# Layer 1 of a hybrid decoder: where k's last sums of squares and the pairs' preparation stand among the projections

## The chip, the cores and the metric

The kernel runs on one core of one Trainium2 chip. The metric is the device time of one execution in microseconds (us). Engines are named as the profile names them: PE multiplies matrices (PEld is its loading of weights), DVE, ACT and POOL work elementwise on the on-chip memory, SP issues the transfers between that memory and the chip's main memory. Each engine takes its instructions in one fixed order; an instruction that waits holds all that stands behind it on its engine.

## What is computed

The reference is a trunk of two layers over 512 tokens of width 2048, in float32. The change lies in layer 1, whose first part is this:

```python
xr = x + xx * mu[0]; xk = x + xx * mu[2]; xg = x + xx * mu[5]   # also xw, xv, xa; xx is the token before, minus x
r = (xr @ w_r); k = (xk @ w_k); v = (xv @ w_v); g = (xg @ w_g)
w_log = -softplus(-(w0 + tanh(xw @ w1) @ w2)) - 0.5
decay = exp(-exp(w_log))
a = sigmoid(a0 + (xa @ a1) @ a2)
kk = (k * k_k).reshape(B_, S, H, N)
kk = kk / max(sqrt(sum(kk * kk, axis=-1)), L2_EPS)
k = k * (1.0 + (a - 1.0) * k_a)
o = wkv7_scan(r, decay, k, v, kk, a)      # 32 heads of 64
bonus = sum(r * k * r_k, axis=-1) * v
```

A norm over o, a gate with silu(g), an output projection and a layer norm follow.

## The kernel before

Every float32 matrix is held as two parts: a rounded one (`hi`, made by ACT, L137) and the rest (`lo`, made by DVE, L138). A product of two such matrices is three PE products (L142 to L144).

**Projections.** `gemm_a` makes 256 columns of a projection (a block): four units of weights, each 512 KB, loaded into `wraw` and split into `whi` and `wlo`, and for each of the 16 slices of x 2 x 3 products of 128x512, so 96 products in a block. The two halves of a block collect in two accumulators `ga` and are taken out by the function `evac` at its end. After each of the four units `pump()` takes one piece of other work from the list `self.side`. k, r and g take eight blocks each, in that order; then v's projection runs inside the scan.

**Mixes.** Each projection reads its own mixture of x with the token before (`mx`, 16 tiles, one buffer each). A mixture is two steps on ACT and two on DVE in turn: scale (L599), add (L600), round (L137), rest (L138). The tiles of the next projection take the buffers of the last one, so mixture i for r can be written only when k's last block has read its own mixture i. With `feed` they are made in the first block of a projection as written, and ahead of it where the engines have time.

**k.** For each half block (a pair of heads, 16 in all) `ev_k` copies the accumulator to `spill`, stores it, squares it (`sq`), splits the square (`sqr`), and puts on the side list a piece that adds it with two products into `ssq`, one row for each head. `self.flush()` runs what is left of the list when k's blocks are written. Beside k's blocks lie two more things: the first factors of w and a (`low`, `loa`, from mixtures `ml`), and `token_layout`, 16 pieces in which POOL scales and shifts a tile of layer 0's output (`xr`, L666 and L667) for a later stage; they are held back until the block before them has been taken out (`gate`).

**Preparation.** After `ssq` DVE makes 1/norm (`rsykk`), stores it as `rn_d`, and `prep(p)` prepares the scan's operands of one pair: it loads k, the norm and the weights `w2`, splits the weights (`w2h`), makes six products (`prew`, `prea`), and goes through ACT and DVE (from `pL`, the running sum, to `rkr`) to two results, which are stored as `ar_d` and `bk_d`. A second part, after `yield`, adds two products (`pb`) and stores `bc_d`. All of its tiles lie in the pool `gph`.

**Order.** The framework's scheduler sets the order on every engine, by what is ready in its own reckoning and by the order in which the code is written; in the scan PE's order is that of the code.

Of the kernel before, what the change touches and what calls it, by code (L numbers as in the profile page):

```python
# [8 lines left out]
F32 = mybir.dt.float32  # L9
# [8 lines left out]
P = 128  # L18
S = 512
# [15 lines left out]
class Kernel:  # L35
# [568 lines left out]
    def layer1(self, x1, x1_ctx, xhat_d, x1_d):  # L604

        nc, tc, i = self.nc, self.tc, self.i
# [22 lines left out]
        hid, lps = {}, {}  # L629
        with tc.tile_pool(name="kph", bufs=1) as kp:  # L630
# [37 lines left out]
                nc.sync.dma_start(x1_d[t * P:(t + 1) * P, sl], r)  # L668

            for c in range(8):  # L670
                if c > 1:
                    with tc.issue_after(gate[0].ins):
                        for q in range((c - 2) * 16 // 6, (c - 1) * 16 // 6):
                            token_layout(q % 4, q // 4)
                self.gemm_a(i["od_w_k"][0], c * 256, m, lambda n, ps: ev_k(c, n, ps), feed=feed)
                ks = [k for k in range(NK) if k * 6 // NK == c]
                for nm, j, w in (("w", 1, i["od_w1"][0]), ("a", 4, i["od_a1"][0])):
                    if not ks:
                        continue
                    nk = len(ks)  # L680
                    wr = kp.tile([P, 3, 96], F32, tag="l1r", name="l1r")[:, :nk]
                    nc.sync.dma_start(wr, w[ks[0] * P:(ks[-1] + 1) * P, :].rearrange("(k p) n -> p k n", p=P))
                    wh = kp.tile([P, 2, 3, 96], F32R, tag="l1h", name="l1h", bufs=2)[:, :, :nk]
                    self.split(wh[:, 0], wh[:, 1], wr)

                    def add(ks=ks, nm=nm, wh=wh, ml=list(self.mixes(kp, tp, x1, j, ks, "ml", 5))):
                        for kk, k in enumerate(ks):
                            self.mm3(lps[nm], wh[:, 0, kk, :], wh[:, 1, kk, :], ml[kk][:, 0, :], ml[kk][:, 1, :],
                                     k == 0, k == NK - 1)

                    self.side.append(add)
            self.flush()
            for nm in "wa":
                h = hid[nm] = hp.tile([96, 2, S], F32R, name="hid" + nm)
                if nm == "w":
                    t = tp.tile([96, S], F32, tag="sp", name="th", bufs=2)
                    nc.scalar.activation(t, lps[nm], AF.Tanh)
                    self.split(h[:, 0, :], h[:, 1, :], t)
                else:
                    self.split(h[:, 0, :], h[:, 1, :], lps[nm])  # L700
            m, feed = [], self.mixes(mp, tp, x1, 0)
            for h in range(2):
                sl = slice(h * 256, h * 256 + 256)
                sm = kp.tile([32, 256], F32, tag="ssm", name="ssm")
                nc.vector.tensor_scalar(sm, ss[:32, sl], 1e-30, None, ALU.max)
                rn = self.rsqrt(kp, sm, 0.0, 256, f"kk{h}", rows=32)
                nc.vector.tensor_scalar(rn, rn, 1.0 / L2_EPS, None, ALU.min)
                nc.sync.dma_start(rn_d[:, sl], rn)
        with tc.tile_pool(name="gph", bufs=1) as gp:

            rt = {}

            def ev_r(p, ps):
                rt[p] = gp.tile([P, S], F32, tag="pr", name="pr", bufs=3)
                nc.scalar.copy(rt[p], ps)

            last = None
            for c in range(8):
                self.gemm_a(i["od_w_r"][0], c * 256, m, lambda n, ps: ev_r(2 * c + n, ps), feed=feed)
                for p in (2 * c, 2 * c + 1):  # L720
                    pr = self.prep(gp, p, rt[p], hid, k_d, rn_d, ar_d, bk_d, bc_d)
                    self.side += [lambda pr=pr: next(pr), lambda pr=last: pr and next(pr, None)]
                    last = pr

            m, feed = [], self.mixes(mp, tp, x1, 5)

            def ev_g(c, n, ps):
                th = tp.tile([P, S], F32, tag="sp", name="gth", bufs=2)
                nc.scalar.activation(th, ps, AF.Tanh, scale=0.5)
                nc.vector.scalar_tensor_tensor(th, th, 1.0, ps, ALU.add, ALU.mult)  # L730
                nc.sync.dma_start(g_d[2 * c + n], th)

            wg = i["od_w_g"][0]
            self.side.append(lambda: next(last, None))
            self.gemm_a(wg, 0, m, lambda n, ps: ev_g(0, n, ps), feed=feed)
            self.flush()
        swp = self.lctx.enter_context(tc.tile_pool(name="swp", bufs=2, side="right"))
        ld_ctx = self.ctx.enter_context(ExitStack())
        ld = ld_ctx.enter_context(tc.tile_pool(name="ld", bufs=1, side="right"))
        for c in range(1, 8):  # L740
            self.gemm_a(wg, c * 256, m, lambda n, ps: ev_g(c, n, ps))
        xv, feed = [], self.mixes(mp, tp, x1, 3)
        self.ps_ctx.close()
        self.wp, self.ww = swp, 512
# [12 lines left out]
    def prep(self, tp, p, r, hid, k_d, rn_d, ar_d, bk_d, bc_d):  # L757
# [30 lines left out]
        iP = tw  # L788
        nc.scalar.activation(iP, L, AF.Exp, scale=CE)
        nc.gpsimd.tensor_copy(self.pcs[:, p, :].unsqueeze(2), Pi[:, :, 64:65])  # L790
        AR, BK = T("pAR", "pAR", (P, 8, 2, 64), 2), T("pBK", "pBK", (P, 8, 2, 64), 2)

        nc.vector.scalar_tensor_tensor(rn, k, col(self.hv["kk"]), rn, ALU.mult, ALU.mult)
        ia, ir = p % 2, 1 - p % 2
# [513 lines left out]
```

## Time and profile before

| | |
|---|---|
| median of 3 runs | 2136.67 us (2131.53 to 2141.84) |
| the profiled execution | 2133.83 us, its span 2132.1 us |
| PE / DVE / ACT / POOL busy | 96 / 61 / 45 / 13 % of the span |
| k's blocks, r's blocks, g's blocks | about 817 to 1014.5, 1014.5 to 1238.5, 1238.5 to 1420 us |
| scan | from about 1424 us |

A busy PE says little, since products overlap: one lasts 0.39 us and the next starts 0.23 us after it. How many products a stretch holds says more.

### The profile page before, as it was taken

The page shows a single profiled execution, that of the slowest core. Times are in us where ns is not written, and L with a number is a line of the kernel's source. Part 1 is how long each engine was busy: PE and PEld are TensorE (multiplying, and loading weights), DVE is VectorE, ACT ScalarE, POOL GpSimd, SP SyncE. Part 2 cuts the span into 40 slices and gives each one's busy share as a digit, 9 for nine tenths or more (in the row PEclk, how much of TensorE's full clock was granted, in tenths as well). Part 3 has the DMA queues.
Part 4 walks back from the last instruction along what each step waited for, and adds up shares of the span by engine and source line. Part 5 has one row for each costly group of instructions (what it writes and reads, how often), then busy time and mean ns, then how long its engine had stood idle before and what let it go on. Part 6 is the DMA issues. An engine that isn't in the chain of part 4 may idle for free. (4 is left out here: it accounts for less than half of the span.)

```text
span 2132.1 us, 33773 instructions
## 1 busy us (share of the span) xinstructions
PE 2036.6 (96%) x13139; PEld 1645.7 (77%) x13139; DVE 1301.0 (61%) x2557; ACT 954.4 (45%) x1663; POOL 268.9 (13%) x334
## 2 busy tenths in 40 slices
PE   8999999999999998999899989999999999989996
PEld 7888888888888897777688768876667676666786
DVE  5334335445333358666777793368888988987336
ACT  3345345333221138555555672254555555564211
POOL 0000000000000000333000030012333333310003
PEclk9999999999999999999999999999999999999998
DMA  5322222333333343455466665322222332333733
GB/s 190 99 70 79 82 77 65 94 99 99 99 105 113 127 170 123 147 177 157 130 235 215 211 210 189 122 80 63 91 87 89 105 104 68 104 109 100 232 104 114
DMA packets 214031, 262.97 MB, mean 123 GB/s; under 512 B 15768, under 2 KB 161776, under 8 KB 213104
## 3 DMA queue, kind: packets, MB, share of 16 engines
q1 hardware_dynamic: 213872, 260.83, 37.6%
q8 instruction: 103, 1.69, 0.3%
q14 instruction: 56, 0.46, 0.1%
HBM read 214.32 MB, written 46.47 MB: 122 GB/s over the span
## 5 line engine op out<-in xcount | busy, mean ns | idle before, releaser
L138 DVE TENSOR_TENSOR wlo<-wraw,whi 128x1024 fp32r<-128x1024 f32 (+1 forms) x268 | 313.8, 1173 | 487.5 <-ACT whi L137 478.5
L137 ACT CAST whi<-wraw 128x1024 fp32r<-128x1024 f32 (+1 forms) x324 | 303.5, 938 | 563.8 <-PE ga L143 318.7
L143 PE MATMUL ga<-mx,whi 128*128 128x512 f32 x768 | 301.9, 393 | 4.1 <-DVE mx L138 4.1
L142 PE MATMUL ga<-mx,whi 128*128 128x512 f32 x768 | 301.1, 393 | 4.5 <-ACT mx L137 4.5
L142 PE MATMUL ga<-x,whi 128*128 128x512 f32 x768 | 301.0, 392 | 0.0
L144 PE MATMUL ga<-mx,wlo 128*128 128x512 f32 x768 | 301.0, 392 | 0.0
L144 PE MATMUL ga<-x,wlo 128*128 128x512 f32 x768 | 299.5, 390 | 0.4 <-DVE wlo L138 0.4
L143 PE MATMUL ga<-x,whi 128*128 128x512 f32 x768 | 299.1, 390 | 0.0
L490 PE MATMUL gb<-wlo,mixed 128*128 128x512 f32 (+1 forms) x576 | 196.8, 343 | 3.1 <-DVE wlo L138 3.1
L488 PE MATMUL gb<-whi,mixed 128*128 128x512 f32 (+1 forms) x576 | 197.4, 343 | 1.8 <-DVE s L439 1.8
L489 PE MATMUL gb<-whi,mixed 128*128 128x512 f32 (+1 forms) x576 | 196.9, 342 | 0.0
L143 PEld LDWEIGHTS ga<-mx,whi 128*128 128x128 f32 x768 | 145.4, 189 | 38.0 <-DVE mx L138 6.9
L142 PEld LDWEIGHTS ga<-mx,whi 128*128 128x128 f32 x768 | 145.1, 189 | 37.9 <-ACT mx L137 5.9
L144 PEld LDWEIGHTS ga<-mx,wlo 128*128 128x128 f32 x768 | 145.3, 189 | 30.9 <-issue 0.3
L144 PEld LDWEIGHTS ga<-x,wlo 128*128 128x128 f32 x768 | 144.2, 188 | 31.2 <-DVE wlo L138 0.9
L142 PEld LDWEIGHTS ga<-x,whi 128*128 128x128 f32 x768 | 144.3, 188 | 29.4 <-ACT whi L137 0.3
L143 PEld LDWEIGHTS ga<-x,whi 128*128 128x128 f32 x768 | 144.3, 188 | 29.1
L490 PEld LDWEIGHTS gb<-wlo,mixed 128*128 128x128 f32 x576 | 109.1, 190 | 16.8 <-DVE wlo L138 4.4
L488 PEld LDWEIGHTS gb<-whi,mixed 128*128 128x128 f32 x576 | 109.1, 190 | 16.0 <-DVE s L439 3.5
L489 PEld LDWEIGHTS gb<-whi,mixed 128*128 128x128 f32 x576 | 109.2, 190 | 12.4
L142 PE MATMUL vps<-mx,whi 128*128 128x512 f32 x256 | 113.3, 443 | 0.0
L138 POOL TENSOR_TENSOR wlo<-wraw,whi 128x512 fp32r<-128x512 f32 x56 | 74.4, 1328 | 256.6 <-ACT whi L137 234.2
(330 smaller groups left out, 3401.0 us busy)
## 6 DMA issues: line engine op xcount, KB each, us to landing
wraw<-in_ev_w_in SPq DMA_DIRECT2D x96, 512.0 KB, 3.6
wraw<-in_ev_w_out SPq DMA_DIRECT2D x32, 512.0 KB, 3.6
wraw<-in_od_w_k SPq DMA_DIRECT2D x32, 512.0 KB, 4.9
wraw<-in_od_w_r SPq DMA_DIRECT2D x32, 512.0 KB, 4.5
wraw<-in_od_w_g SPq DMA_DIRECT2D x32, 512.0 KB, 3.4
wraw<-in_od_w_v SPq DMA_DIRECT2D x64, 256.0 KB, 2.8
ar_d<-pAR SPq DMA_DIRECT2D x16, 512.0 KB, 2.6
bk_d<-pBK SPq DMA_DIRECT2D x16, 512.0 KB, 3.3
```

What stands on the lines that cost most here:

```text
L137: self.nc.scalar.copy(hi, src)
L138: (eng or self.nc.vector).tensor_sub(lo, src, hi.bitcast(F32))
L142: mm(ps, ah, bh, start=start, stop=False)
L143: mm(ps, ah, bl, start=False, stop=False)
L144: mm(ps, al, bh, start=False, stop=stop)
L488: mm(ps, ah, bh, start=start, stop=False)
L489: mm(ps, al, bh, start=False, stop=False)
L490: mm(ps, ah, bl, start=False, stop=stop)
```

## The change

- The list is no longer flushed after k's last block. What is left of it, the two sums of squares of pairs 14 and 15, is taken by the first two pumps of r's first block. r's first block is written before the norm, so `ev_r` keeps tiles 0, 1, 12 and 13 in a pool that is open longer.
- `token_layout` runs in five blocks of k (c = 2 to 6) instead of six (c = 2 to 7).
- The pairs' preparation is spread out. Before, each block of r put two preparations on the list for the next block, in the order prepare p, finish p-1 with no pause, so that 14 of 16 start in r's blocks 1 to 7 and the last two in g's first block. Now a pair has three places on the list (prepare p, finish p-1, nothing), four of them in each block: r's blocks 1 to 7 start pairs 0 to 9, g's first block takes none, g's blocks 1 to 5 start pairs 10 to 15, and block 6 finishes pair 15.
- The pools for v's weights and for the scan's operands (`swp`, `ld`), which take the place of `gph`, open before g's last block instead of before its second.
- To make room: `pAR` and `pBK` have one buffer instead of two, `ml` four instead of five, `pr` five and two instead of three.

```diff
             for c in range(8):
-                if c > 1:
+                if 1 < c < 7:
                     with tc.issue_after(gate[0].ins):
-                        for q in range((c - 2) * 16 // 6, (c - 1) * 16 // 6):
+                        for q in range((c - 2) * 16 // 5, (c - 1) * 16 // 5):
                             token_layout(q % 4, q // 4)
...
-                    def add(ks=ks, nm=nm, wh=wh, ml=list(self.mixes(kp, tp, x1, j, ks, "ml", 5))):
+                    def add(ks=ks, nm=nm, wh=wh, ml=list(self.mixes(kp, tp, x1, j, ks, "ml", 4))):
...
-            self.flush()
+
             for nm in "wa":
+                assert not self.side[2:]
...
+            rt = {}
+
+            def ev_r(p, ps):
+                pool, bufs = (tp, 2) if p in (0, 1, 12, 13) else (gp, 5)
+                rt[p] = pool.tile([P, S], F32, tag="pr", name="pr", bufs=bufs)
+                nc.scalar.copy(rt[p], ps)
+
+            gp = None
             m, feed = [], self.mixes(mp, tp, x1, 0)
+            self.gemm_a(i["od_w_r"][0], 0, m, lambda n, ps: ev_r(n, ps), feed=feed)
+            self.flush()
             for h in range(2):
...
-            last = None
-            for c in range(8):
-                self.gemm_a(i["od_w_r"][0], c * 256, m, lambda n, ps: ev_r(2 * c + n, ps), feed=feed)
-                for p in (2 * c, 2 * c + 1):
-                    pr = self.prep(gp, p, rt[p], hid, k_d, rn_d, ar_d, bk_d, bc_d)
-                    self.side += [lambda pr=pr: next(pr), lambda pr=last: pr and next(pr, None)]
-                    last = pr
+            prs = {}
+
+            def prep(p):
+                prs[p] = self.prep(gp, p, rt[p], hid, k_d, rn_d, ar_d, bk_d, bc_d)
+                next(prs[p])
+
+
+            steps = []
+            for p in range(16):
+                steps += [lambda p=p: prep(p), lambda p=p: p and next(prs[p - 1], None), lambda: None]
+            for c in range(1, 8):
+                self.side += steps[4 * c - 4:4 * c]
+                self.gemm_a(i["od_w_r"][0], c * 256, m, lambda n, ps: ev_r(2 * c + n, ps))
...
             wg = i["od_w_g"][0]
-            self.side.append(lambda: next(last, None))
             self.gemm_a(wg, 0, m, lambda n, ps: ev_g(0, n, ps), feed=feed)
-            self.flush()
+            for c in range(1, 7):
+                self.side += steps[4 * c + 24:4 * c + 28] if c < 6 else [lambda: next(prs[15], None)]
+                self.gemm_a(wg, c * 256, m, lambda n, ps: ev_g(c, n, ps))
         swp = self.lctx.enter_context(tc.tile_pool(name="swp", bufs=2, side="right"))
         ld_ctx = self.ctx.enter_context(ExitStack())
         ld = ld_ctx.enter_context(tc.tile_pool(name="ld", bufs=1, side="right"))
-        for c in range(1, 8):
-            self.gemm_a(wg, c * 256, m, lambda n, ps: ev_g(c, n, ps))
+        self.gemm_a(wg, 7 * 256, m, lambda n, ps: ev_g(7, n, ps))
...
-        AR, BK = T("pAR", "pAR", (P, 8, 2, 64), 2), T("pBK", "pBK", (P, 8, 2, 64), 2)
+        AR, BK = T("pAR", "pAR", (P, 8, 2, 64)), T("pBK", "pBK", (P, 8, 2, 64))
```

What the change does to the order on three engines follows. First PE, where r's first block begins. `ga0` and `ga1` are the two halves of that block, `sqr_7628` is the split square of pair 14. Before, nine products of r stand ahead of these rows:

```order
L142 MATMUL ga1_7701<-mx_7720,whi_7704 128x512
L649 MATMUL ssq_5948<-sqr_7628,selr_5943 32x512
L143 MATMUL ga1_7701<-mx_7720,whi_7704 128x512
L144 MATMUL ga1_7701<-mx_7720,wlo_7705 128x512
L142 MATMUL ga0_7700<-mx_7726,whi_7704 128x512
L143 MATMUL ga0_7700<-mx_7726,whi_7704 128x512
L649 MATMUL ssq_5948<-sqr_7628,selr_5943 32x512
```

The first of the two products of pair 14 is the eleventh on PE after k's last product. Now it stands behind r's first unit of weights, and both products together:

```order
L142 MATMUL ga1_7649<-mx_7680,whi_7652 128x512
L143 MATMUL ga1_7649<-mx_7680,whi_7652 128x512
L144 MATMUL ga1_7649<-mx_7680,wlo_7653 128x512
L649 MATMUL ssq_5948<-sqr_7628,selr_5943 32x512 x2
L142 MATMUL ga0_7648<-mx_7718,whi_7658 128x512
```

24 products of r go ahead of it instead of 10; those of pair 15 follow after 24 more. On ACT and DVE the rows around `sqr` of pairs 14 and 15 stand in the same order as before.

Second POOL, at the end of k's blocks: `gate` is the tiny copy that marks the end of a half block, so two of them end a block. Before:

```order
L641 COPY gate<-spill 128x1 x2
L666 TENSOR_TENSOR xr<-xr,lng 128x512 x2
L667 TENSOR_TENSOR xr<-xr,lnb 128x512 x2
L666 TENSOR_TENSOR xr<-xr,lng 128x512
L667 TENSOR_TENSOR xr<-xr,lnb 128x512
L641 COPY gate<-spill 128x1 x2
L786 MEMSET pPi 128x8
```

Three tiles of `token_layout` lie between the gates of k's blocks 6 and 7, which is during block 7. Now:

```order
L666 TENSOR_TENSOR xr<-xr,lng 128x512
L667 TENSOR_TENSOR xr<-xr,lnb 128x512
L666 TENSOR_TENSOR xr<-xr,lng 128x512
L667 TENSOR_TENSOR xr<-xr,lnb 128x512
L641 COPY gate<-spill 128x1 x4
L797 MEMSET pPi 128x8
```

The gates of the last two blocks follow each other: POOL has nothing to do during block 7.

Third DVE, in g's first block, at the last four of g's mixtures (`mxf` from x_12 to x_15). Before:

```order
L600 SCALAR_TENSOR_TENSOR mxf<-x_12_4405,vec_234,mxf 128x512
L802 TENSOR_TENSOR pBK<-pk,ptw 128x8x64
L805 SCALAR_TENSOR_TENSOR pr<-pr,vec_246,pk 128x512
L138 TENSOR_TENSOR mx<-mxf,mx 128x512
L600 SCALAR_TENSOR_TENSOR mxf<-x_13_4406,vec_234,mxf 128x512
L138 TENSOR_TENSOR rkr<-pr,rkr 128x512
L600 SCALAR_TENSOR_TENSOR mxf<-x_14_4407,vec_234,mxf 128x512
L138 TENSOR_TENSOR mx<-mxf,mx 128x512
L600 SCALAR_TENSOR_TENSOR mxf<-x_15_4408,vec_234,mxf 128x512
L138 TENSOR_TENSOR wlo<-wraw,whi 128x1024
L784 SCALAR_TENSOR_TENSOR pL<-rst,ptw 128x512
L138 TENSOR_TENSOR mx<-mxf,mx 128x512 x2
```

Pair 14's preparation ends among them, and pair 15's (`pL`) begins ahead of the last two mixtures. Now:

```order
L813 TENSOR_TENSOR pBK<-pk,ptw 128x8x64
L816 SCALAR_TENSOR_TENSOR pr<-pr,vec_246,pk 128x512
L138 TENSOR_TENSOR wlo<-wraw,whi 128x1024
L138 TENSOR_TENSOR rkr<-pr,rkr 128x512
L138 TENSOR_TENSOR mx<-mxf,mx 128x512
L600 SCALAR_TENSOR_TENSOR mxf<-x_13_4406,vec_234,mxf 128x512
L600 SCALAR_TENSOR_TENSOR mxf<-x_14_4407,vec_234,mxf 128x512
L600 SCALAR_TENSOR_TENSOR mxf<-x_15_4408,vec_234,mxf 128x512
L138 TENSOR_TENSOR mx<-mxf,mx 128x512 x3
```

Here it is pair 9's preparation that ends ahead of them, and no other begins before the last mixture is done.

## Rows read from the trace of the kernel before

**Rows 1.** The page: busy time, share of the span and instructions of each engine; DVE's busy share and PE's granted clock in 40 equal slices of the span, in tenths; and the transfer of a unit of g's weights (size, median time from issue to landing).

```profile
PE 2036.6 (96%) x13139; PEld 1645.7 (77%) x13139; DVE 1301.0 (61%) x2557; ACT 954.4 (45%) x1663; POOL 268.9 (13%) x334
DVE  5334335445333358666777793368888988987336
PEclk9999999999999999999999999999999999999998
wraw<-in_od_w_g SPq DMA_DIRECT2D x32, 512.0 KB, 3.4
```

**Rows 2.** Busy time by stretch of the span. Columns: stretch, its length, then busy time and number of instructions of PE, PEld, DVE, ACT and POOL, the granted clock of PE, the share of the DMA engines, GB/s. The stretches: k's blocks before the last; k's last block; the beginning of r's first block; r's blocks up to 1180; r's last blocks and g's first; g's other blocks.

```profile
821.00:992.00 171.00, 170.20 (x744) 134.68 (x743) 116.05 (x129) 96.91 (x154) 45.66 (x39) 1.00 0.49 153
992.00:1016.90 24.90, 24.88 (x110) 19.83 (x108) 22.54 (x24) 16.57 (x27) 9.96 (x7) 1.00 0.46 148
1016.90:1030.70 13.80, 5.95 (x19) 4.37 (x20) 11.48 (x17) 13.53 (x22) 0.97 (x2) 0.75 0.34 115
1030.70:1180.00 149.30, 149.30 (x656) 122.88 (x655) 108.30 (x160) 76.45 (x122) 2.87 (x19) 1.00 0.60 202
1180.00:1273.00 93.00, 83.19 (x338) 63.20 (x337) 81.33 (x116) 67.60 (x112) 20.24 (x13) 0.98 0.61 209
1273.00:1424.00 151.00, 151.00 (x667) 125.03 (x666) 62.60 (x76) 52.60 (x72) 2.85 (x3) 1.00 0.41 134
```

**Rows 3.** Who PE waited for between 1180 and 1280 us: line of the waiting product, what it waited for, us in total, times, longest.

```profile
PE ga L143 <- DVE mx L138: 3.8, 4, 1.8
PE pb L811 <- DVE rkr L138: 2.3, 5, 0.6
PE pb L811 <- ACT rkr L137: 1.5, 2, 1.3
PE prew L144 <- DVE w2h L138: 1.4, 2, 1.1
PE ga L142 <- ACT mx L137: 0.6, 2, 0.5
```

**Rows 4.** PE in order of time at the beginning of r's first block: start, duration, line, operation; in brackets the idle time before it and what ended it.

```profile
1016.49 0.39 PE L142 MATMUL ga<-mx,whi 128*128 128x512 f32 x1
1024.75 0.64 PE L649 MATMUL ssq<-sqr,selr 128*32 128x512 f32 x1 [7.88 <-ACT sqr L137]
...
1028.60 0.40 PE L144 MATMUL ga<-mx,wlo 128*128 128x512 f32 x1
```

**Rows 5.** The same columns as in rows 2, for the two stretches in this part of the span in which the granted clock is at the lower of its two levels.

```profile
1021.80:1028.60 6.80, 3.85 (x10) 2.82 (x11) 5.67 (x9) 6.80 (x13) 0.97 (x2) 0.50 0.49 163
1250.40:1253.90 3.50, 3.50 (x10) 2.69 (x10) 3.50 (x8) 3.50 (x8) 3.50 (x1) 0.51 0.40 156
```

**Rows 6.** ACT in order of time, on the way to pair 14's split square.

```profile
1022.08 0.58 ACT L639 COPY spill<-ga 128x512 f32<-128x512 f32 x1
...
1024.07 0.63 ACT L137 CAST sqr<-sq 128x512 fp32r<-128x512 f32 x1
```

**Rows 7.** DVE in order of time from k's last block on; x2 or x3 are rows of one kind back to back, and the time is that of all.

```profile
996.68 3.20 DVE L138 TENSOR_TENSOR mx<-mxf,mx 128x512 fp32r<-128x512 f32 x2 [2.36 <-ACT mx L137]
999.81 1.78 DVE L138 TENSOR_TENSOR sqr<-sq,sqr 128x512 fp32r<-128x512 f32 x1
1001.52 1.79 DVE L600 SCALAR_TENSOR_TENSOR mxf<-x,vec,mxf 128x512 f32<-128x512 f32 x1
...
1006.83 4.17 DVE L600 SCALAR_TENSOR_TENSOR mxf<-x,vec,mxf 128x512 f32<-128x512 f32 x3
...
1025.36 0.68 DVE L138 TENSOR_TENSOR sqr<-sq,sqr 128x512 fp32r<-128x512 f32 x1
```

**Rows 8.** POOL in order of time in k's last block.

```profile
996.33 3.01 POOL L666 TENSOR_TENSOR xr<-xr,lng 128x512 f32<-128x512 f32 x2
999.30 3.46 POOL L667 TENSOR_TENSOR xr<-xr,lnb 128x512 f32<-128x512 f32 x2
1006.98 1.76 POOL L666 TENSOR_TENSOR xr<-xr,lng 128x512 f32<-128x512 f32 x1 [4.22 <-DMA xr<-xhat_d]
1008.82 1.64 POOL L667 TENSOR_TENSOR xr<-xr,lnb 128x512 f32<-128x512 f32 x1
```

**Rows 9.** DVE's groups of instructions between 1054 and 1275 us, which holds all 16 preparations: count, busy us, mean ns of one, idle time before them and what ended it. `wlo`, `mx` and `mxf` are no part of a preparation. `pL` and `w2h` are the first and the last of the eleven groups of a preparation by time (16 instructions in each; together 126.7 us).

```profile
L138 DVE TENSOR_TENSOR wlo<-wraw,whi 128x1024 fp32r<-128x1024 f32 x33 | 40.2, 1219 | 2.5 <-ACT whi L137 2.4
L784 DVE TENSOR_TENSOR_SCAN pL<-rst,ptw 128x512 f32<-128x512 f32 x16 | 19.5, 1219 | 0.6 <-ACT ptw L782 0.6
...
L138 DVE TENSOR_TENSOR mx<-mxf,mx 128x512 fp32r<-128x512 f32 x16 | 10.5, 678 | 0.0
L600 DVE SCALAR_TENSOR_TENSOR mxf<-x,vec,mxf 128x512 f32<-128x512 f32 x14 | 10.3, 741 | 0.0
L138 DVE TENSOR_TENSOR w2h<-w,w2h 96x256 fp32r<-96x256 f32 x16 | 6.4, 398 | 0.0
```

**Rows 10.** DVE in order of time at the first preparation.

```profile
1053.41 0.75 DVE L793 SCALAR_TENSOR_TENSOR pn<-pk,hkk,pn 128x512 f32<-128x512 f32 x1 [4.10 <-DMA pn<-rn_d]
...
1055.21 0.41 DVE L138 TENSOR_TENSOR w2h<-w,w2h 96x256 fp32r<-96x256 f32 x1
```

**Rows 11.** The last `ml` tiles for one block, on DVE, and the first product that reads them, on PE, in order of time.

```profile
878.53 1.29 DVE L138 TENSOR_TENSOR ml<-mxf,ml 128x512 fp32r<-128x512 f32 x2
883.04 0.39 PE L142 MATMUL loa<-ml,l1h 128*96 128x512 f32 x1
```

More of the change, by code (lines that the diff above doesn't have):

```diff
@@ L709, in layer1 @@
         with tc.tile_pool(name="gph", bufs=1) as gp:
[L711 to L715, printed above, removed]
-            last = None
-            for c in range(8):
-                self.gemm_a(i["od_w_r"][0], c * 256, m, lambda n, ps: ev_r(2 * c + n, ps), feed=feed)
-                for p in (2 * c, 2 * c + 1):
-                    pr = self.prep(gp, p, rt[p], hid, k_d, rn_d, ar_d, bk_d, bc_d)
-                    self.side += [lambda pr=pr: next(pr), lambda pr=last: pr and next(pr, None)]
-                    last = pr
+            prs = {}
[8 more added lines that the diff above has]
+                self.gemm_a(i["od_w_r"][0], c * 256, m, lambda n, ps: ev_r(2 * c + n, ps))
             m, feed = [], self.mixes(mp, tp, x1, 5)
```

## The prediction, made before the changed kernel ran

> **What bounds the kernel now.** The first look is at the page's shares: PE is busy 96% of the span [rows 1], so what can be won is PE's waits, and a change off PE counts only where PE waits for it. The second look divides layer 1's projections into stretches and counts products. From 1030.7 to 1180 PE starts 656 products in 149.3 us, 0.2276 us each, and waits for nothing [rows 2]. By that pace the other stretches are measured: k's last block and g's blocks from 1273 on hold as many products as they can (110 and 667). Two stretches fall short. From 1016.9 to 1030.7 there are 19 products in 13.8 us: 13.8 - 19 x 0.2276 = 9.5 us lost. From 1180 to 1273 there are 338 in 93.0 us: 16.1 us lost. These 25.6 us are all that this change can win.
>
> The third look is at who is waited for. In the first stretch it is one wait of 7.88 us of PE for ACT's split square of pair 14, followed by products at the slow pace until 1028.60 [rows 4]; the granted clock reads 0.50 there, the lower of its two levels, 1.2 GHz, after PE had stood idle [rows 5]. Nine starts in 3.85 us cost 1.8 us more than at full clock, so 9.5 is 7.7 of wait and 1.8 of clock. In the second stretch PE waits for DVE and ACT in three places: g's mixtures (`mx`), `pb`, and the preparation's weights (`w2h`), 9.6 us in all [rows 3]; the rest of the 16.1 are restarts and another stretch at low clock [rows 5]. There DVE is busy 81.33 of 93.0 us, against 62.60 of 151 in g's other blocks [rows 2]: DVE is late, and has room later.
>
> **The change part by part.**
>
> *The sums of squares move behind r's first unit.* PE comes to pair 14's first product after 24 products of r instead of 10, so 14 x 0.2276 = 3.2 us later: at 1019.9 instead of 1016.7, to the second at 1020.1. Before, its `hi` part is ready at 1024.70 [rows 6] and `lo` at 1026.04 [rows 7]. With nothing else moved PE would still wait 5.9 us, and this edit alone would give about 1.8.
>
> *POOL is taken out of k's last block.* ACT's copy that starts pair 14's square comes at 1022.08, though k's products were done before 1015: ACT has no idle time ahead of it, it works off r's mixtures [rows 6], in turn with DVE, which is busy 22.54 of 24.9 us [rows 2]. And DVE is slow in that block just where POOL works [rows 7, 8]: two `mx` take 3.20 us where the mean is 0.678 each [rows 9], `sqr` 1.78 where it takes 0.68 later, one `mxf` 1.79 and three 4.17 where one takes 0.741. The excess is 1.84 + 1.10 + 1.05 + 1.95 = 5.9 us. Without POOL it goes, and as DVE and ACT hand each mixture back and forth twice, ACT's copy comes earlier by the same. `lo` is then ready at 1020.1, when PE asks for it. I take 0.3 us of wait as left and none of the low clock: 9.2 us won. The bounds: 1.8 if nothing of the 5.9 reaches ACT, 9.5 if all does.
>
> The Trainium skill (SBUF — State Buffer, Who interferes with whom) says more than this row: DVE with two inputs from this memory and a reading POOL instruction exclude each other, and the loser stands still for the whole instruction. By that, POOL's 9.9 us of rows 8 would be what DVE gets back, not 5.9, and pair 14 would be ready some 4 us before PE comes. The rows show DVE stretched, by 5.9, so I stay with these; the rule would only make the wait's end safer.
>
> The pieces taken out of block 7 go to the blocks before it, which get three or four instead of two or three. DVE is busy 116.05 of 171 us there, with POOL's 45.66 beside it, and PE is busy 170.20 [rows 2]. `ml` with four buffers instead of five: the last `ml` are done at 879.8, and the product that reads them starts at 883.04 [rows 11]. 3 us cover it; without them the price would be up to one `ml` chain, 2.8 us, in each of six blocks. I take nothing for both.
>
> *The preparation is spread.* Its DVE work is 126.7 us for 16 pairs [rows 9], 7.9 each. In r's last block and g's first, DVE has to do, before, four pairs, 16 mixtures at 0.678 + 0.741 and eight `wlo` at 1.219: 31.7 + 22.7 + 9.8 = 64.2 us. PE's products there are 192 and 32 for the pairs, 51.0 us. DVE is 13 us over, and the stretch loses 16.1: this is that loss. Now two pairs fall into these blocks, 8 and 9: 15.8 + 22.7 + 9.8 = 48.3 us against 206 products, 46.9 us. The means count twice where instructions follow each other closely (two `ml` in 1.29 us [rows 11], not 1.36), so DVE just fits. I take 1.5 us as left: 14.6 won. The bounds are 0 and 16.1.
>
> *The preparation in g's blocks.* Six pairs, 47.5 us, come to the 62.6 us that DVE does in 151 us: 73%. That is the share of r's first blocks (108.3 of 149.3), in which PE lost nothing [rows 2]. The queue of SP takes the pairs' loads and stores with them; the DMA engines are at 0.41 there and at 0.60 in r's blocks. I take 0.5 us lost; upper bound, what `pb` and `w2h` cost between 1180 and 1280: 2.3 + 1.5 + 1.4 = 5.2 us [rows 3].
>
> *The first pair.* Its norm starts at the last sum of squares, which comes 4 to 5 us earlier; PE asks for `w2h` after 153 products of r instead of 130, so 9.2 - 23 x 0.2276 = 4.0 us earlier. `w2h` stands on DVE behind `pn`, which waited 4.10 us for a transfer [rows 10]. The two move alike; I take 0.5 us, bounds 0 and 4.1.
>
> *At nothing:* one buffer of `pAR` and `pBK`, as a pair now comes every three pumps, 3 x 24 products or 16 us, and its store lands long before; the copies `pr`, of which one (pair 11's) waits on ACT for pair 6's `rkr`, while PE goes on with the other two accumulators; and the later pools, see the last rival.
>
> **The sum.** 9.2 + 14.6 - 0.5 - 0.5 = 22.8 us. The profiled execution took 2133.83 us, so it would take 2111.0. The median of the three runs lies 2.8 us above that execution: 2136.67 - 22.8 = 2113.9. I say 2114.
>
> **The rivals.**
>
> *B: the wait for the squares stays.* ACT reaches the copy late for another reason than POOL: r's mixtures wait for k's last block to release their buffers. For it: the order on ACT and DVE is unchanged there. Against it: the buffers are free when PE ends that block, before 1015, and ACT still comes at 1022. Then 1.8 is won there, in all 15.4: 2121.
>
> *C: r's end stays as it is.* Pair 9's preparation still stands among g's mixtures, and each mixture goes twice between ACT and DVE; if their handing over and not DVE's load is what makes g wait, nothing is won in the second stretch: 9.2 - 0.5 = 8.7 won, 2128. Half of it would be 2121.
>
> *D: the waits move into g's blocks,* at the price of rows 3, 5.2 us and as much again for restarts and clock: 12 won, 2124 at worst, 2119 likelier.
>
> *E: slower.* The loads of v's first weights, of `AR` and of `BK` now stand behind pair 15's last store, and the last unit of g's weights behind v's in SP's queue. Pair 15's `pb` comes after the first unit of g's block 6. From there to the product that needs that last unit are 6 x 24 products, 32.8 us; the store, the load of 3.4 us [rows 1] and its split (1.22 on DVE [rows 9], about as much on ACT) need some 10. So 22 us are spare. If the preparation falls further behind than that, each further us delays g's end and the scan; slower by 0.5% needs it 22 + 23 + 11 = 56 us late, more than two blocks. With DVE at 73% I see no cause.
>
> **How the numbers follow.** The forecast, 2108 to 2119, has 0.64; B 0.12, C 0.12, D 0.08, E 0.04. What a measurement of this kernel can tell from no change is about 0.5%, 10.7 us, so faster is below 2126. The forecast, B, D and a quarter of C are: 0.87. Same: the rest of C, 0.09. Slower: E. For the range, the low end is all 25.6 won and 6 us for other runs of the same kernel (the three differ by 10): 2105. The high end takes in B, D and half of C: 2127.
>
> **What the changed profile would show.** PE's wait for `sqr` gone or under 1 us, and no low clock near r's first block; ACT's copy of pair 14 within 3 us of k's last product; DVE's `mx` in k's last block at 0.7 us, POOL idle there; the stretch around g's first block at 0.2276 us a product, with waits for `mx` under 2 us; g's blocks without waits for `pb`. Wrong would be: a wait of 5 us for `sqr` (B), `mx` waits of 4 us (C), waits for `pb` or `w2h` between g's blocks (D), or an idle PE ahead of the scan (E).

## The result and the profile after

The changed kernel takes 2114.26 us (median of 4 runs, 2112.11 to 2116.03), the kernel before, beside it, 2137.39 us. The ratio is 0.9887, with a 95% interval from 0.9869 to 0.9905: 20 to 28 us faster. The profiled execution took 2116.03 us, its span is 2114.3 us.

One measure is used from here on, **the stretch**: from r's first product to the first product of the scan. In every trace it holds 1686 products, which at the pace of the prediction (0.2276 us) take 383.7 us; what is above that is lost. Before it runs from 1014.45 to 1424.35, 409.9 us with 26.2 lost. After it runs from 1018.82 to 1405.53, 386.7 us with 3.0 lost. So 23.2 us were won there, where 22.8 were forecast. That the stretch begins 4.4 us later is nothing that the change did: a second profile of the same kernel (below) has it at 1014.52.

The page first, as in [rows 1]; columns are busy time, share of the span, instructions, and then the tenths of 40 slices:

```profile
PE 2032.7 (96%) x13139; PEld 1648.2 (78%) x13139; DVE 1295.1 (61%) x2557; ACT 956.5 (45%) x1663; POOL 250.1 (12%) x334
...
DVE  5334344444433358656866776577888988886336
...
PEclk9999999999999999999999999999999999999998
```

The shares say nothing of the 23 us. The stretches do; columns as in [rows 2], and the places are the same ones: k's last block, the beginning of r's first block, r's blocks, r's end with g's beginning, g's other blocks.

```profile
996.40:1021.30 24.90, 24.90 (x110) 20.17 (x110) 20.83 (x30) 20.15 (x33) 0.18 (x1) 1.00 0.38 126
1021.30:1035.10 13.80, 12.46 (x54) 9.55 (x53) 11.35 (x17) 12.80 (x20) 0.90 (x2) 1.00 0.42 142
1035.10:1164.00 128.90, 128.05 (x562) 105.07 (x561) 82.93 (x123) 59.71 (x91) 2.15 (x14) 1.00 0.57 188
1164.00:1257.00 93.00, 93.00 (x411) 76.79 (x410) 68.39 (x93) 58.75 (x91) 1.34 (x7) 1.00 0.52 174
1257.00:1405.00 148.00, 148.00 (x653) 122.24 (x652) 97.77 (x131) 77.55 (x118) 4.57 (x14) 1.00 0.58 195
```

The second row holds 54 products where the same 13.8 us held 19, the fourth 411 in 93 us where it was 338. The granted clock is 1.00, the higher level of 2.4 GHz, in all five, so the stretches of [rows 5] have no counterpart. POOL is busy 0.18 us in k's last block, where [rows 8] had four rows. All that PE still waits for in the stretch, as in [rows 3], now of the whole of it:

```profile
PE ssq L649 <- DVE sqr L138: 0.9, 1, 0.9
PE prew L142 <- ACT w2h L137: 0.5, 1, 0.5
PE ssq L649 <- ACT sqr L137: 0.4, 1, 0.4
PE prew L144 <- DVE w2h L138: 0.3, 1, 0.3
```

At r's beginning, PE in order of time, against the 7.88 us of [rows 4]:

```profile
1024.03 0.39 PE L144 MATMUL ga<-mx,wlo 128*128 128x512 f32 x1
1024.83 0.42 PE L649 MATMUL ssq<-sqr,selr 128*32 128x512 f32 x1 [0.42 <-ACT sqr L137]
1026.18 0.42 PE L649 MATMUL ssq<-sqr,selr 128*32 128x512 f32 x1 [0.92 <-DVE sqr L138]
```

The way to that square on ACT, from the copy of pair 13 (its first row) to that of pair 14, against [rows 6]:

```profile
1001.22 0.59 ACT L639 COPY spill<-ga 128x512 f32<-128x512 f32 x1 [3.99 <-DMA k_d<-spill]
...
1022.16 0.58 ACT L639 COPY spill<-ga 128x512 f32<-128x512 f32 x1
...
1024.16 0.62 ACT L137 CAST sqr<-sq 128x512 fp32r<-128x512 f32 x1
```

And DVE in k's last block, against [rows 7]:

```profile
1002.36 0.69 DVE L138 TENSOR_TENSOR mx<-mxf,mx 128x512 fp32r<-128x512 f32 x1 [3.67 <-ACT mx L137]
...
1004.06 0.68 DVE L138 TENSOR_TENSOR sqr<-sq,sqr 128x512 fp32r<-128x512 f32 x1
1004.66 0.75 DVE L600 SCALAR_TENSOR_TENSOR mxf<-x,vec,mxf 128x512 f32<-128x512 f32 x1
...
1009.02 2.07 DVE L600 SCALAR_TENSOR_TENSOR mxf<-x,vec,mxf 128x512 f32<-128x512 f32 x3
```

A `mx` takes 0.69 us, a `sqr` 0.68, three `mxf` 2.07, where beside POOL two `mx` took 3.20, a `sqr` 1.78 and three `mxf` 4.17.

### The profile page after: what moved, and what is told of

It is laid out like the page before. It is cut to its first block, busy times and chain, and to the rows that moved or that the text cites. A ratio compares the mean times of both kernels' runs of the same rounds, so it can differ in the third digit from the quotient of the medians.

```text
span 2114.3 us, 33769 instructions
## 1 busy us (share of the span) xinstructions
PE 2032.7 (96%) x13139; PEld 1648.2 (78%) x13139; DVE 1295.1 (61%) x2557; ACT 956.5 (45%) x1663; POOL 250.1 (12%) x334
```

## The experiments

Eleven experiments ran (e11 is the changed kernel once more), each with 4 to 12 runs in the comparison, against the kernel before on the same chip. "Lost" is the stretch less 383.7 us, in the one profiled execution.

| run | edit | median us | ratio to before, 95% | stretch us | lost |
|---|---|---|---|---|---|
| before | | 2137.39 | | 409.9 | 26.2 |
| after | | 2114.26 | 0.9887 (0.9869 to 0.9905) | 386.7 | 3.0 |
| e1 | before, POOL out of k's last block | 2135.67 | 0.9981 (0.9969 to 0.9993) | 403.2 | 19.5 |
| e2 | after, POOL back in it | 2120.75 | 0.9919 (0.9903 to 0.9935) | 392.2 | 8.4 |
| e3 | after, old packing of the pairs | 2130.64 | 0.9962 (0.9947 to 0.9977) | 399.4 | 15.7 |
| e4 | after, g's first block takes its share | 2117.43 | 0.9899 (0.9881 to 0.9917) | 386.1 | 2.3 |
| e5 | after, sums and first pair later | 2111.45 | 0.9886 (0.9873 to 0.9900) | 383.6 | 0 |
| e6 | after, one pair more ahead of g's mixtures | 2118.73 | 0.9918 (0.9905 to 0.9932) | 388.8 | 5.1 |
| e7 | after, two pairs more | 2118.47 | 0.9919 (0.9906 to 0.9933) | 389.8 | 6.0 |
| e8 | after, `token_layout` a block earlier | 2113.86 | 0.9897 (0.9884 to 0.9911) | 383.6 | 0 |
| e9 | e3, `pn` behind its own `pL` | 2117.94 | 0.9907 (0.9891 to 0.9923) | 389.4 | 5.6 |
| e10 | e5 and e8 together | 2111.68 | 0.9881 (0.9860 to 0.9903) | 383.6 | 0 |
| e11 | after, once more | 2112.57 | 0.9881 (0.9865 to 0.9896) | 386.1 | 2.4 |

Times of one kernel lie 2 to 13 us apart from run to run, and the parts that no edit touches differ between traces, layer 0 by up to 4 us and what follows from the scan's first product on by up to 6. So a question of 3 us is settled by the stretch in the trace, and the time must only not contradict it.

### POOL in k's last block (e1, e2)

e1 is the kernel before with this edit alone:

```diff
-                if c > 1:
+                if 1 < c < 7:
                     with tc.issue_after(gate[0].ins):
-                        for q in range((c - 2) * 16 // 6, (c - 1) * 16 // 6):
+                        for q in range((c - 2) * 16 // 5, (c - 1) * 16 // 5):
```

> The kernel before with one edit: POOL's token_layout keeps out of k's last block. Theory (POOL slows DVE in that block, and so pair 14's square): DVE's mx in the block falls from 1.6 to 0.7 us, ACT's copy of pair 14 comes 4 to 6 us earlier, PE's wait of 7.9 us for the split square falls to about 3.6 (ready 4.3 us earlier, as in the changed kernel), 4 to 5.5 us faster, about 2132. Rival (the copy is late because r's mixtures wait for buffers or for one another): the wait stays at 7 to 8 us, no gain, 2137. The page of the skill (whole instructions exclude each other): 9.9 us back, the wait gone, 2128.

PE in order of time in e1:

```profile
1021.38 0.39 PE L142 MATMUL ga<-mx,whi 128*128 128x512 f32 x1
1025.34 0.64 PE L649 MATMUL ssq<-sqr,selr 128*32 128x512 f32 x1 [3.57 <-ACT sqr L137]
```

The wait of 7.88 us is 3.57, and 6.7 us are won in the stretch: 4.8 at r's beginning, as expected, and 1.9 at r's end, where the edit moves nothing (1.6 of these are the slow products at 1250 of [rows 5], which e1's execution doesn't have). The time is 1.5 to 6.6 us shorter. The rival falls: nothing else was moved, and the square is earlier. ACT's copies in e1:

```profile
1001.72 0.59 ACT L639 COPY spill<-ga 128x512 f32<-128x512 f32 x1 [3.97 <-DMA k_d<-spill]
...
1022.66 0.58 ACT L639 COPY spill<-ga 128x512 f32<-128x512 f32 x1
```

From the copy of pair 13 to that of pair 14 it is 20.94 us; before it was 1022.08 - 995.55 = 26.53, with pair 13's copy in this row:

```profile
995.55 0.59 ACT L639 COPY spill<-ga 128x512 f32<-128x512 f32 x1 [2.69 <-DMA k_d<-spill]
```

So ACT gets 5.6 us back, of the 5.9 read from [rows 7]. The Trainium skill (SBUF — State Buffer, Who interferes with whom) lets one of two such instructions stand still for the whole of the other. The trace of the kernel before agrees; POOL and DVE go in turn, here the first rows of [rows 7] and [rows 8] one by one:

```profile
996.33 1.31 POOL L666 TENSOR_TENSOR xr<-xr,lng 128x512 f32<-128x512 f32 x1
996.68 1.50 DVE L138 TENSOR_TENSOR mx<-mxf,mx 128x512 fp32r<-128x512 f32 x1 [2.36 <-ACT mx L137]
997.59 1.75 POOL L666 TENSOR_TENSOR xr<-xr,lng 128x512 f32<-128x512 f32 x1
998.11 1.78 DVE L138 TENSOR_TENSOR mx<-mxf,mx 128x512 fp32r<-128x512 f32 x1
```

POOL's first takes 1.31 us, as long as one alone. The `mx` that starts during it ends 0.54 us after it (998.18 against 997.64), POOL's second 1.16 us after that `mx`, the next `mx` 0.55 us after POOL's second. What does not hold is the size that the prediction and the expectation drew from the rule, POOL's 9.9 us of [rows 8]: these rows hold POOL's own waiting for DVE as well, and DVE is held up in six instructions, by 0.8 to 1.1 us each.

e2 is the changed kernel with this edit undone.

> The changed kernel with one edit undone: token_layout lies in six blocks again, k's last among them. Theory: pair 14's split square comes 4 to 6 us later, PE, which asks for it 24 products into r's first block, waits about 6 us instead of 1.3 and some products run at the low clock: 5 to 6 us slower than the changed kernel, about 2120. Rival (the moved sums alone do it): 2114 to 2115, wait under 2 us.

PE in order of time in e2:

```profile
1026.04 0.63 PE L649 MATMUL ssq<-sqr,selr 128*32 128x512 f32 x1 [5.01 <-ACT sqr L137]
1027.38 0.64 PE L649 MATMUL ssq<-sqr,selr 128*32 128x512 f32 x1 [0.71 <-DVE sqr L138]
```

5.7 us of wait, and the products behind it start 0.43 us apart, at a granted clock of 0.51, the lower level: 5.4 us slower than the changed kernel in the stretch. At r's beginning the kernel before loses 9.8 us over the steady pace, e2 (the order alone) 8.6, e1 (POOL alone) 5.0, the changed kernel 1.7. One edit alone is worth 1.2 or 4.8, both together 8.1. The 2.1 on top are mostly the low clock: its slow products cost 1.8 us before, 2.3 in e2, 1.3 in e1, and nothing in the changed kernel, since either wait alone still brings it on.

### Why r's end was slow (e3, e4, e6, e7, e9)

e3 takes the pauses out of the list again, starts the last two pairs in g's first block, and gives `pr` and `pAR` their old numbers of buffers (the cut shows the list alone):

```diff
-                steps += [lambda p=p: prep(p), lambda p=p: p and next(prs[p - 1], None), lambda: None]
+                steps += [lambda p=p: prep(p), lambda p=p: p and next(prs[p - 1], None)]
...
+            self.side += steps[28:] + [lambda: next(prs[15], None)]
             self.gemm_a(wg, 0, m, lambda n, ps: ev_g(0, n, ps), feed=feed)
+            self.flush()
```

> The changed kernel with the preparation packed as before: two pairs to each block of r, the last two in g's first block, and pr with three buffers and pAR with two. Theory (DVE has 64.2 us to do against 51.0 of PE at r's end and g's beginning): the waits for mx, pb and w2h come back there, 14 to 16 us slower than the changed kernel, about 2129. Rival (those waits came from the late norm, which is earlier by 4 to 5 us now): at most 10 us come back, 2124 or less. In either case nothing is lost at r's beginning.

12.7 us more are lost than in the changed kernel, a little under the 14 to 16 expected, and the ratios lie 16 us apart. PE's waits in e3 from 1100 us on are those of [rows 3] again, without `w2h`:

```profile
PE ga L143 <- DVE mx L138: 3.1, 3, 1.7
PE ga L142 <- ACT mx L137: 2.1, 2, 1.8
PE pb L823 <- ACT rkr L137: 1.3, 1, 1.3
PE pb L823 <- DVE rkr L138: 1.2, 2, 0.6
```

So the packing is the cause, and the earlier norm is not (its rival allowed at most 10). e4 and the two after it ask whether it is DVE's load in r's last and g's first block, as the prediction had it. In e4 g's first block takes its share, so that pair 10 starts in it:

```diff
-            self.gemm_a(wg, 0, m, lambda n, ps: ev_g(0, n, ps), feed=feed)
-            for c in range(1, 7):
-                self.side += steps[4 * c + 24:4 * c + 28] if c < 6 else [lambda: next(prs[15], None)]
-                self.gemm_a(wg, c * 256, m, lambda n, ps: ev_g(c, n, ps))
+            for c in range(7):
+                self.side += steps[4 * c + 28:4 * c + 32] + [lambda: next(prs[15], None)] * (c == 5)
+                self.gemm_a(wg, c * 256, m, lambda n, ps: ev_g(c, n, ps), feed=None if c else feed)
```

> The changed kernel, but g's first block takes its share of the preparation too (pair 10 starts in it, and all later pairs come one block earlier): three pairs start in r's last and g's first block instead of two. Theory (DVE's load there decides): 23.7 + 22.7 + 9.8 = 56.2 us of DVE against 216 products, 49.2 us, so PE loses 7 to 8.5 us at mx, pb and w2h: about 2122. Rival (what cost 16 us before was the backlog of two pairs in every block of r, not the load of these two blocks): under 2 us lost, 2114 to 2116.

Nothing is lost in the trace (386.1 us), and the expectation fails. It was badly aimed too: pair 10 is taken by that block's third pump, and DVE comes to it only after g's last mixture, when nothing waits. The profiled execution is also the fastest of the six (2110.69 us, the median 2117.43), so the trace speaks for that one alone. e6 takes pair 10 at the block's first pump, and e7 pair 11 at its third. This is e7; in e6 the second line has `steps[30:32]` alone, and in both the later pairs move up to match:

```diff
-                self.side += steps[4 * c - 4:4 * c]
+                self.side += steps[4 * c - 4:4 * c] if c < 7 else steps[24:26] + steps[27:29]
...
+            self.side += steps[30:32] + steps[33:35]
             self.gemm_a(wg, 0, m, lambda n, ps: ev_g(0, n, ps), feed=feed)
```

> The changed kernel with pair 10's preparation taken by the first pump of g's first block (pair 9's one place earlier), so that its DVE work lies ahead of g's last mixture, with PE's 8 products. In the changed kernel g's mixtures 12 to 15 are ready 2.1 to 3.6 us before PE asks. Theory (DVE's work up to the last mixture decides): 7.9 of DVE less 1.8 of PE less that lead is 2.5 to 4 us lost, the stretch from r's first product to the scan 389 to 391 us instead of 386.7, about 2118. Rival (no loss without a backlog from r's earlier blocks): under 1 us, 387.5 or less.

> As the run with one pair more, and pair 11 in g's first block as well: four pairs start in r's last and g's first block, as many as in the kernel before, but r's blocks 1 to 6 hold only their eight. The sum of the prediction (64.2 us of DVE against 51.0 of PE) gives 13 to 16 us lost, the stretch 400 to 403. The lead of the mixtures gives less, since pair 11 only begins ahead of the last mixture: 7.9 + 2.3 - 1.8 - 2.8 = 5.6 us and 1 to 2 for pb behind them, 392 to 395. If the backlog of r's earlier blocks made the loss: 388 or less.

e6 loses 2.3 us around g's first block, just under the 2.5 to 4 of its expectation: one pair more eats up the mixtures' lead and a little over. e7 loses 3.4 us there, less than either reckoning by load and a little more than none. It has four pairs in the two blocks, exactly as many as e3 and the kernel before, and loses less than a third of the 11.9 us that e3 loses there. PE's waits in e7:

```profile
PE ga L143 <- DVE mx L138: 1.8, 2, 1.0
...
PE ga L142 <- ACT mx L137: 0.8, 1, 0.8
```

So the load of these two blocks is not the main reason; something was brought along from r's earlier blocks. The kernel before shows it. There DVE starts pair 2's `pL` 5.2 us after PE's first `prew` of that pair, pair 6's 8.9 us, pair 10's 13.0 us: it falls behind by about 1 us a pair, though it is idle for a quarter of r's blocks (108.30 us busy of 149.30, [rows 2]). First DVE, then SP, in order of time in the middle of r's blocks (1170.89 is pair 8, 1178.58 and 1184.75 are pair 9, the `pn` at 1176.77 is already pair 10's):

```profile
1170.89 0.74 DVE L805 SCALAR_TENSOR_TENSOR pr<-pr,vec,pk 128x512 f32<-128x512 f32 x1
...
1176.77 0.75 DVE L793 SCALAR_TENSOR_TENSOR pn<-pk,hkk,pn 128x512 f32<-128x512 f32 x1 [3.40 <-DMA pk<-k_d]
...
1178.58 1.22 DVE L784 TENSOR_TENSOR_SCAN pL<-rst,ptw 128x512 f32<-128x512 f32 x1
...
1184.75 0.75 DVE L805 SCALAR_TENSOR_TENSOR pr<-pr,vec,pk 128x512 f32<-128x512 f32 x1
```

```profile
1171.92 0.74 SPq L765 DMA_DIRECT2D pk<-k_d  x1
```

This is a closed loop. `pk` has two buffers. The `pr` of pair 8 is the last to read one of them; only then can SP load pair 10's k into it, which lands 4.9 us after its issue; DVE has pair 10's `pn` ahead of pair 9's `pL`, and waits for that load with all that stands behind; then pair 9 runs to its own `pr`, which frees the buffer for pair 11. A round takes 1184.75 - 1170.89 = 13.9 us. PE gives a pair 56 products, 12.75 us. After a dozen pairs the preparation is some 11 us late, and g's mixtures, which stand among the last pairs, are late with it.

e9 leaves the old packing of e3, its loads and its DVE work as they are and takes `pn` out of the loop:

```diff
-        nc.vector.tensor_tensor_scan(L, self.rst.rearrange("p a b -> p (a b)"), tw, 0.0, ALU.mult, ALU.add)
+        scan = nc.vector.tensor_tensor_scan(L, self.rst.rearrange("p a b -> p (a b)"), tw, 0.0, ALU.mult, ALU.add)
...
-        nc.vector.scalar_tensor_tensor(rn, k, col(self.hv["kk"]), rn, ALU.mult, ALU.mult)
+        with tc.issue_after(scan.ins):
+            nc.vector.scalar_tensor_tensor(rn, k, col(self.hv["kk"]), rn, ALU.mult, ALU.mult)
```

> The run with the old packing (two pairs in each block of r) with one edit: a pair's pn on DVE is held back until its own pL, so that pn of the next pair no longer stands ahead of this pair's pL. Theory (with the old packing each pair's chain closes a loop: the last read of pk on DVE, then SP's load of the next pk into that buffer, 4.9 us, then pn, then pL; 13.9 to 14.1 us a round against 12.8 us of PE, so the preparation falls behind by about 1 us a pair): the delay from prew to pL stays at 3 to 5 us over all pairs instead of growing from 4.6 to 12.3, the loss around g's first block falls from 12.7 us to 3 to 5, the stretch from r's first product to the scan from 399.4 to 390 to 392 us, the time from 2130.6 to about 2121. Rival (the sum of the prediction: DVE has 13 us too much to do there): the stretch stays at 398 to 400, 2129.

The stretch is 389.4 us: 10.0 of the 12.7 us come back with this one edit, a little more than expected, and the ratio falls from 0.9962 to 0.9907. `pL` starts 2.9 us after `prew` for every pair from 3 to 11. DVE in order of time in e9:

```profile
1184.67 0.74 DVE L818 SCALAR_TENSOR_TENSOR pr<-pr,vec,pk 128x512 f32<-128x512 f32 x1
...
1191.22 1.23 DVE L796 TENSOR_TENSOR_SCAN pL<-rst,ptw 128x512 f32<-128x512 f32 x1 [0.60 <-ACT ptw L794]
1192.36 0.73 DVE L806 SCALAR_TENSOR_TENSOR pn<-pk,hkk,pn 128x512 f32<-128x512 f32 x1
...
1197.44 0.74 DVE L818 SCALAR_TENSOR_TENSOR pr<-pr,vec,pk 128x512 f32<-128x512 f32 x1
```

`pn` waits for nothing, the round is 12.77 us, PE's own pace. The groups of waits of DVE from 1054 to 1230 us say it for all pairs; e3 has

```profile
DVE pn L805 <- DMA pk<-k_d: 23.8, 9, 3.6
```

and e9 has no such row; its longest is the wait for the next weights, which is what an engine with room shows:

```profile
DVE wlo L138 <- ACT whi L137: 23.6, 15, 4.2
```

The changed kernel has the loop too (its `pn` still waits for `pk`), but a pair now comes every 80 products, 18.2 us, and a round of 14 fits. A third buffer for `pk`, which by this account should open the loop as well, was not tried.

One smaller wait has another origin. In g's first block of the kernel before, POOL's copy of 128x8 elements, 0.19 us in its median, lasts as long as DVE runs 21 operations without a pause, and ends 0.06 us after the last of them:

```profile
1250.04 14.76 POOL L790 COPY pcs<-pPi 128x8 f32<-128x8 f32 x1 [11.48 <-ACT pPi L787]
```

ACT waits 2.27 us for it with pair 15's `pPi`, and DVE 0.82 us behind that; PE's wait of 1.3 us for `pb` on ACT in [rows 3] comes at the end of pair 15's chain, and costs 1.5 us with its restart. e3 has the same copy (14.78 us) and the same wait; in e9 the copy takes 7.79 us and that wait is gone.

### The last 3 us (e5, e8, e10, e11)

e5 moves the four products into `ssq` to the second pump, and the first pair two places back:

```diff
+            both = self.side[:]
+            self.side[:] = [lambda: None, lambda: [f() for f in both]]
...
+            steps[:3] = steps[2::-1]
```

> The changed kernel with both kinds of sums that PE still waits for moved later: all four products into ssq at the second pump of r's first block (48 products in, so the norm starts no later), and the first pair's preparation two places later. Theory (what is left of loss between r's first product and the scan, 3 us of waits for sqr and w2h, is only a matter of what PE asks for too early): no wait for sqr, none or one under 0.3 us for w2h, that stretch 383.8 us in the trace instead of 386.7, the time 2111 to 2112. Rival (the first pair's chain moves along with its place, or the second pair's w2h is late instead): a wait of 1 us stays, 385 to 386.

e8 moves `token_layout` instead (`0 < c < 6` for `1 < c < 7`, with c - 1 and c in place of c - 2 and c - 1).

> The changed kernel with token_layout in k's blocks 1 to 5 instead of 2 to 6. Theory (the stores of token_layout's last two tiles stand ahead of pair 12's store on SP's queue and delay the copy of pair 13 by 1.3 us, and with it the chain to pair 14's square): ACT's wait for that store is back at 2.7 us from 4.0, pair 14's square 1.3 us earlier against r's first product, PE's wait for sqr 0.3 us or less instead of 1.34, the stretch from r's first product to the scan 385.6 instead of 386.7; the time cannot tell it from 2114. Rival (the transfer itself is slower for another reason): the wait stays at 1.3 us.

Both have no wait of PE left in the stretch, e5 as expected (383.6 us), e8 better than expected (383.6, not 385.6). In the changed kernel the last two stores of `token_layout` hold SP's queue ahead of pair 12's store:

```profile
991.18 2.94 SPq L668 DMA_DIRECT2D x_d<-xr  x2
994.21 0.39 SPq L151 DMA_DIRECT2D wraw<-in_od_w_k  x1
994.65 0.57 SPq L151 DMA_DIRECT2D wraw<-in_od_w_r  x1
995.28 0.50 SPq L640 DMA_DIRECT2D k_d<-spill  x1
```

That store holds the buffer in which pair 13 is copied, and ACT waits 3.99 us (shown above), 1.3 us longer than in the kernel before. Only 0.5 us of this is the issue itself, 0.57 us after the copy of pair 12 where before it came at once. The other 0.8 us is the transfer, 5.9 us from issue to landing instead of 5.1, now with two loads of weights, 512 KB each, issued just ahead of it: the two stores held these up too. In e8 no load is issued just ahead, the store lands 2.0 us after its issue, and ACT's copy of pair 13 follows without idle time. That it is these loads that make the transfer longer fits all three, but was not tested apart. ACT in e8:

```profile
992.50 0.59 ACT L639 COPY spill<-ga 128x512 f32<-128x512 f32 x1 [5.38 <-PE ga L144]
...
995.50 0.59 ACT L639 COPY spill<-ga 128x512 f32<-128x512 f32 x1
```

The expectation took back 1.3 us of that wait; all of it went, and the first pair's wait with it, since the norm starts earlier too.

> The changed kernel with the two edits together that each took its last waits away in the trace: the later places for the sums of squares and the first pair, and token_layout one block earlier. Theory (that stretch holds as many products as it can in either): nothing more is won there, 383.6 us, the time that of the run with the later places, 2111 to 2112. Rival (the two add up): 382.5 or less.

> The changed kernel itself, unaltered, beside the two others on the same chip: 2114, the stretch from r's first product to the scan 386.7 us as in its first profile, and the waits for sqr and w2h (3 us) in the same places; if these waits are another execution's chance, they are gone or elsewhere.

Together they give the same 383.6 us, all that the stretch can:

```profile
1015.50:1399.20 383.70, 383.70 (x1690) 316.22 (x1688) 260.01 (x359) 207.41 (x317) 8.94 (x37) 1.00 0.55 185
```

(e10, columns as in [rows 2]: PE is busy without a gap.) e11 repeats the changed kernel: waits in the same places, 2.4 us lost. In time e5 and e10 are not told apart from the changed kernel (2111.45 and 2111.68 against 2114.26 and 2112.57, with overlapping intervals); that they are 2.5 to 3 us better is the trace's word.

## Why the prediction was right, and where it was not

**The time** was forecast at 2114 and is 2114.26, the stretch's gain at 22.8 and is 23.2. Three of its four terms are off in size by 0.5 to 1.1 us, and the largest came out 1.5 us higher than forecast, for a wrong reason. The four errors, -1.1, +1.5, +0.5 and -0.9 us, cancel: that the time is hit to 0.3 us is luck, and e11 gives the same kernel 2112.57.

**k to r: 9.2 forecast, 8.1 measured** (1.7 left instead of 0.3). The order's share of about 1.8 was 1.2 (e2). POOL's 5.9 us were 5.6 on ACT's way between the two copies (e1). The term mis-sized is the start of that way: the pieces moved to block 6 end with two stores ahead of pair 12's on SP, and ACT's copy of pair 13 waits 3.99 us instead of 2.69. So the square came 4.3 us earlier, not 5.9. The step that failed is "*I take nothing for both*", the price of the moved pieces: it counted DVE and `ml`, and not the queue of SP, on which each piece puts a load and a store. Also "ACT's copy of pair 14 within 3 us of k's last product" was missed, by half a microsecond, and PE's wait for `sqr`, "gone or under 1 us", is 1.3 us in two pieces. Rival B is dead by e1.

**r to g: 14.6 forecast, all 16.1 won, for another reason.** The step that failed is the reckoning of 64.2 us of DVE against 51.0 of PE, "13 us over, and the stretch loses 16.1: this is that loss". e7 and e9 have as many pairs, mixtures and `wlo` in those two blocks and lose 3.4 and 2.6 us there. Most of the loss was the backlog of the loop through `pk`: in e3, 9.3 of the 11.9 us around g's first block go when `pn` leaves the loop. What e7 and e9 still lose is the most that can be put down to the load. For the kernel before itself the loop is read from its rows; e9's edit was not made in it. That loop could have been read before the run: where PE already waits, between 1182 and 1207, DVE is not full.

```profile
1182.00:1207.00 25.00, 23.84 (x103) 18.71 (x102) 17.71 (x23) 13.58 (x22) 0.42 (x3) 1.00 0.63 215
```

(The kernel before, columns as in [rows 2]: DVE busy 17.71 of 25 us.) PE waits there for `pb` and `w2h` of DVE, and an engine that is waited for while it is idle is itself waiting; DVE's own waits name `pk`. The sum also took all four pairs as due ahead of the last mixture, and pair 15 ends behind it. Rival C, the handing over between ACT and DVE, was nearer in kind, since a chain and not a load was at work, but it was another chain, and not one that stays: the pauses give it room.

**g's blocks: 0.5 forecast, 0 measured.** DVE is busy 66% there and PE waits for nothing. D and E did not come; how much further back the preparation could stand before E bites was not tried.

**The first pair: 0.5 forecast, 1.4 measured** with the restarts. The step that failed is "Its norm starts at the last sum of squares, which comes 4 to 5 us earlier": against r's first product, pair 14's square came 4.3 us earlier, but the last sum, pair 15's, stands behind 24 more products and came 2.9 us earlier (16.2 us after r's first product before, 13.3 now). DVE began the norm only 1.4 us earlier, as it was busy with other work, while PE asks for `w2h` 2.9 us earlier. The chain also stands behind a transfer for which `pn` waited 4.10 us before [rows 10] and now, on DVE:

```profile
1056.13 0.75 DVE L804 SCALAR_TENSOR_TENSOR pn<-pk,hkk,pn 128x512 f32<-128x512 f32 x1 [5.06 <-DMA pn<-rn_d]
```

## What to carry to other kernels

Before an engine's load is made the cause of a wait, look whether it is idle in that stretch, and what it waits for: a busy sum that happens to match the loss proves nothing. Follow a repeated piece of work round by round: the delay of its nth round against the engine that feeds it tells a backlog (it grows) from a burst (it doesn't), and a buffer that is freed late, reloaded and read ahead of turn makes a loop whose length can be read off between two equal rows. And when work is moved, move its loads and stores in the head too: a store that waits on a queue can cost an engine that has nothing to do with it.

## What the runs showed of the hardware

- DVE's 128x512 operations with two inputs from on-chip memory take 0.68 to 0.75 us alone, and 1.50 to 1.79 us while POOL multiplies or adds tiles of the same size; POOL's take 1.29 to 1.31 us alone and 1.64 to 1.76 us beside them. The two go in turn, one of each in 1.7 us. Six such DVE operations in k's last block cost 5.6 us on the way that they lie on.
- A wait of PE of 3.57 us (e1) was followed by products 0.43 us apart, at a granted clock of 0.50, the level of 1.2 GHz; two waits of 0.42 and 0.92 us in the changed kernel were not. The slow products cost 1.3 us behind that wait, and 2.3 us behind the 5.0 and 0.7 us of e2. The length of the wait alone does not tell: a wait of 1.76 us in g's first block of the kernel before was followed by the stretch at 1250.40 of [rows 5], while two of 1.74 us there in e1 were not followed by slow products.
- A POOL copy of 128x8 elements, 0.19 us in its median, took 14.76 us (the kernel before), 14.78 (e3) and 13.57 us (e7) while DVE ran 21, 21 and 19 operations without a pause, most of them with two inputs from on-chip memory, and ended 0.06 us after the last of them. There POOL got no turn, unlike its 128x512 operations in k's last block.
